# An encoder layer with a product-key expert FFN on one Trainium2 core: the first G load moved to GpSimd's queue, SyncE in written order in the main loop, the next U split ahead of the gathers

## The chip, the cores and the metric

The kernel runs on one core of one Trainium2 chip. The metric is the time of one execution in microseconds on the device. The engines are TensorE (PE; its weight loads are PEld), VectorE (DVE), ScalarE (ACT), GpSimd (POOL) and SyncE (SP), which here only issues DMAs. Line numbers such as L923 are those of the kernel before.

## The reference

One encoder layer for 512 tokens of width 1024: neighbourhood attention and latent attention, a projection and LayerNorm, and then the part that the change touches, a FFN of 128 x 128 experts of which each token takes 16 for each of 8 heads.

```python
def one_chunk(xb):                      # 128 tokens
    q = (xb @ w_q).reshape(PEER_CHUNK, PEER_HEADS, PEER_KEY_DIM)
    s1 = jnp.einsum('thd,kd->thk', q[..., :half], sub_keys[0])
    s2 = jnp.einsum('thd,kd->thk', q[..., half:], sub_keys[1])
    ...                                 # top 16 of the sums: expert numbers idx, weights g
    u = u_table[idx]
    hpre = jnp.einsum('td,ted->te', xb, u)
    act = g * jax.nn.gelu(hpre, approximate=False)
    return jnp.einsum('te,ted->td', act, v_table[idx])
...
h = layer_norm(DN_ALPHA * h + ffn + ple, ln2_g[i], ln2_b[i])
```

## The kernel before

The 16,384 experts are handled as 128 blocks of 128. Tokens 128 to 511 (384 of them) are computed densely: every block's V rows are multiplied with a matrix of activations that is zero where a token did not choose the expert. The routing weights of these tokens, spread out over all experts, are the matrix G, which an earlier stage (`build_g`) writes to DRAM as `g_dram`. Tokens 0 to 127 are computed sparsely, by gathering rows of U and V.

**Ahead of the main loop** (until about 770 us) `route` finds the experts of each token, `build_g` writes G, and a filler computes the first 44 (LEAD) blocks of `expert_in`: the U block of 128 experts is loaded (`raw`, three buffers, L630) and multiplied with 320 tokens (L632, 16 records for each block in full float32), and ScalarE applies Gelu into `ge` (L634). For a while after that, `i_sel` (L776) holds the expert numbers of the sparse tokens.

**The main loop** (L986) goes over the 128 blocks in the order 24 to 127, then 0 to 23; n counts the steps. In a step:
- `expert_in(n + LEAD)` while n + 44 < 128: `stream` loads a U block into `raw` (L87), `split` makes a high part `whi` on ScalarE (L79) and a low part `wlo` on VectorE (L80), both with two buffers, and TensorE runs 24 matmuls of 128x320 into `hp` (two buffers). Gelu follows on ScalarE.
- `load_g` every 8 steps (GB), at n % 8 == 4: one DMA (L923) brings G for eight blocks, 1536 KB, into `gt0` or `gt1` in turn. The first such load, `load_g(0)`, is written ahead of the loop (L933). Its rows in DRAM are cut into runs of 512 bytes, 3072 of them (128 partitions x 24).
- `load_v(n)` loads a V block of 512 KB into `v_raw` (three buffers, L929), and `split` makes `v_hi` and `v_lo`.
- VectorE multiplies G with `ge` in place (L1013), and `split` makes `a_hi` and `a_lo`. For the last 24 steps `ge` comes back from DRAM as `ge_in` (L1008).
- `expert_out`: 18 matmuls of 128x512 into six accumulators `acc` that live through the whole loop.
- Two or three of the 257 gather steps: an indirect DMA of 128 rows by GpSimd into `gat` (six buffers) and one VectorE operation on it (`scr`, L955, for U; `base`, L966, for V). `spent` counts steps, 0.25 for each step without an `expert_in`, so that the gather steps are spread evenly up to n = 115.

After the loop the four row blocks are normalised and stored (L1034 to L1042). Row block 0, the sparse one, is ready when its last gather is, so its normalisation is placed by the planner inside the loop.

**The order of the work.** The program is compiled with a planner that estimates when each instruction can run and orders the instructions of each engine by that. Inside `tc.manual_schedule(engines={...})` the engines named keep the order in which the code is written; before, this is VectorE alone. TensorE, ScalarE, SyncE and GpSimd follow the planner. Each engine then executes its list in order, and an instruction that waits holds up everything behind it on its engine.

In what follows u42 is the load of the U block with number 42 in that sequence (the filler's last two are u42 and u43, the loop's first is u44), W44 the VectorE half of the split of block 44, v3 and V3 the load and the VectorE half of the split of the V block of step 3, gt3 the product in place, A3 the VectorE half of the split of the activations, G0 the first G load and G1 the next, and g one gather's VectorE operation.

Of the kernel before, what the change touches and what calls it, by code (L numbers as in the profile page):

```python
# [32 lines left out]
GT = 16  # L33
GB = 8
LEAD = 44
# [7 lines left out]
NA_KEYS = 256  # L43
NA_FROM = (0, 64, 192, 256)
GATS = 6
LOW = -3.0e38
FEED_NA = 2.75
FEED_LAT = 1.0
# [7 lines left out]
def tile_encoder_layer(ctx: ExitStack, tc: tile.TileContext, A: dict, out: bass.AP):  # L56
    nc = tc.nc
# [15 lines left out]
    def r32(ap):  # L73
        return ap.bitcast(F32)

    def split(hi, lo, src, scale=None):

        if scale is None:
            nc.scalar.copy(hi, src)  # L79
            nc.vector.tensor_tensor(lo, src, r32(hi), op=OP.subtract)  # L80
        else:
            nc.scalar.mul(hi, src, scale)
            nc.vector.scalar_tensor_tensor(lo, src, scale, r32(hi), op0=OP.mult, op1=OP.subtract)

    def stream(src, shape, scale=None):
        raw = wst.tile([128] + shape, F32, name="raw", bufs=3)
        nc.sync.dma_start(raw, src)  # L87
        hi = wst.tile([128] + shape, F32R, name="whi")
        lo = wst.tile([128] + shape, F32R, name="wlo")
        split(hi, lo, raw, scale)  # L90
        return hi, lo

    def mm3(ps, a, b, start, stop):
        nc.tensor.matmul(ps, a[0], b[0], start=start, stop=False)  # L94
        nc.tensor.matmul(ps, a[0], b[1], start=False, stop=False)  # L95
        nc.tensor.matmul(ps, a[1], b[0], start=False, stop=stop)  # L96
# [85 lines left out]
    def soft(s_in, p, nk, mx, scale=1.0, minus=-1.0):  # L182

        nmx = small.tile([128, 1], F32, name="nmx")
        nc.vector.tensor_scalar(nmx, mx, minus, None, op0=OP.mult)
        sm = small.tile([128, 1], F32, name="sm")
        nc.scalar.activation(p[:, :nk], s_in, AF.Exp, bias=nmx, scale=scale, accum_out=sm)
        rs = small.tile([128, 1], F32, name="rs")
        nc.vector.reciprocal(rs, sm)
        nc.vector.tensor_scalar(p[:, :nk], p[:, :nk], rs, None, op0=OP.mult)  # L190
# [52 lines left out]
    with tc.tile_pool(name="ln0", bufs=1, reuse_waits="tile") as ln0:  # L243
# [5 lines left out]
        for c in range(4):  # L249
            layer_norm(h[c], eg, eb)  # L250
            transpose_to(hTh, hTl, h[c], c)
            if c == 0:
                for kk in range(4):
                    raw = wst.tile([128, 2, 512], F32, name="raw", bufs=3)
# [141 lines left out]
    def na_scores(m, b, hh):  # L396
# [9 lines left out]
        nc.vector.tensor_tensor_reduce(p[:, :NA_KEYS], ps[:, :NA_KEYS], bias, op0=OP.add, op1=OP.max,  # L406
                                       accum_out=mx, scale=1.0, scalar=LOW)
        soft(p[:, :NA_KEYS], p, NA_KEYS, mx)
# [203 lines left out]
    g_dram = dram.tile([NTG, 128, 128 * GT], F32, name="g_dram")  # L612
# [7 lines left out]
    def expert_in(i, whole=None):  # L620


        ps = psH.tile([128, 512], F32, name="hp")
        if whole is None:
            u = stream(A["uT"][i], [8, 128])
            for k in range(8):
                mm3(ps[:, :N_U], (u[0][:, k], u[1][:, k]), (hTh[:, k, ts], hTl[:, k, ts]), k == 0, k == 7)
        else:
            u = wst.tile([128, 8, 128], F32, name="raw", bufs=3)
            nc.sync.dma_start(u, A["uT"][i])  # L630
            for k in range(8):
                nc.tensor.matmul(ps[:, :N_U], u[:, k], whole[:, k, :], start=(k == 0), stop=(k == 7))  # L632
        ge = pB.tile([128, N_U], F32, name="ge", bufs=LEAD - SPILL + 2)
        nc.scalar.activation(ge, ps[:, :N_U], AF.Gelu)  # L634
        if i < SPILL:
            nc.sync.dma_start(ge_dram[i], ge)
        else:
            ge_t[i] = ge
# [14 lines left out]
    def top16(vals, idx, src, tmp):  # L653
        nc.vector.max(vals[:, 0:8], src)
        nc.vector.max_index(idx[:, 0:8], vals[:, 0:8], src)
        nc.vector.match_replace(tmp, vals[:, 0:8], src, LOW)
        nc.vector.max(vals[:, 8:16], tmp)
# [258 lines left out]
    order = list(range(SPILL, 128)) + list(range(SPILL))  # L916
    pV = ctx.enter_context(tc.tile_pool(name="pV", bufs=1, side="right", reuse_waits="tile"))

    def load_g(n):
        i = order[n]  # L920
        t = pV.tile([128, NTG, GB, GT], F32, name="gt0") if n // GB % 2 == 0 else pE.tile([128, NTG, GB, GT], F32,
                                                                                          name="gt1", bufs=1)
        nc.sync.dma_start(t.rearrange("p g i t -> p g (i t)"),  # L923
                          g_dram[:, :, i * GT:(i + GB) * GT].rearrange("g p x -> p g x"))
        return t

    def load_v(n):
        raw = pV.tile([128, D], F32, name="v_raw", bufs=3)
        nc.sync.dma_start(raw, v_rows[order[n] * 128:(order[n] + 1) * 128, :])  # L929
        return raw  # L930

    v_next = [load_v(n) for n in range(2)]
    gt_next = load_g(0)  # L933
    v_next.append(load_v(2))
    for c in range(NGC):
        for _ in route(c, []):
# [14 lines left out]
    def gather_u(c, k):  # L951
        u = pG.tile([128, D], F32, name="gat", bufs=GATS)
        nc.gpsimd.indirect_dma_start(out=u[:], out_offset=None, in_=u_rows,  # L953
                                     in_offset=bass.IndirectOffsetOnAxis(ap=i_sel[:, c, k:k + 1], axis=0))
        nc.vector.scalar_tensor_tensor(scr, u, 1.0, h[c], op0=OP.mult, op1=OP.mult,  # L955
                                       accum_out=hdot[:, c, k:k + 1])
# [5 lines left out]
    def gather_v(c, k):  # L962
        u = pG.tile([128, D], F32, name="gat", bufs=GATS)
        nc.gpsimd.indirect_dma_start(out=u[:], out_offset=None, in_=v_rows,  # L964
                                     in_offset=bass.IndirectOffsetOnAxis(ap=i_sel[:, c, k:k + 1], axis=0))
        nc.vector.scalar_tensor_tensor(base[c], u, hdot[:, c, k:k + 1], base[c], op0=OP.mult, op1=OP.add)  # L966

    def gather_steps():
        for c in range(NGC):
            for k in range(128):  # L970
                yield lambda c=c, k=k: gather_u(c, k)
            yield lambda c=c: gather_act(c)
            for k in range(128):
                yield lambda c=c, k=k: gather_v(c, k)

    def expert_out(x, c, halves=(0, 1)):
        n, ah, al, vh, vl = x
        cs = slice(c * 128, (c + 1) * 128)
        for hf in halves:
            hs = slice(hf * 512, (hf + 1) * 512)  # L980
            mm3(acc[c][hf], (ah[:, cs], al[:, cs]), (vh[:, hs], vl[:, hs]), n == 0, n == 127)

    steps = list(gather_steps())
    done, spent = 0, 0
    late = []
    with tc.manual_schedule(engines={nc.vector.engine}):  # L986
        for n, i in enumerate(order):
            if n + LEAD < 128:
                expert_in(n + LEAD)
            if n % GB == 0:  # L990
                gt = gt_next
            if n % GB == GB // 2 and n + GB // 2 < 128:
                gt_next = load_g(n + GB // 2)
            raw = v_next[n] if n < 3 else load_v(n)
            if n in (124, 125):
                vh = wst.tile([128, D], F32R, name="whi")
                vl = wst.tile([128, D], F32R, name="wlo")
                a2 = wst.tile([128, 2, N_D], F32R, name="raw", bufs=3)
                ah, al = a2[:, 0], a2[:, 1]
            else:  # L1000
                vh = pP.tile([128, D], F32R, name="v_hi")
                vl = pP.tile([128, D], F32R, name="v_lo")
                ah = pP.tile([128, N_D], F32R, name="a_hi")
                al = pP.tile([128, N_D], F32R, name="a_lo")
            split(vh, vl, raw)
            if i < SPILL:
                ge = pG.tile([128, N_U], F32, name="ge_in", bufs=2)
                nc.sync.dma_start(ge, ge_dram[i])  # L1008
            else:
                ge = ge_t.pop(i)  # L1010
            a = gt[:, :, n % GB, :]
            dn = gt[:, N_S // GT:, n % GB, :]
            nc.vector.tensor_tensor(dn, dn, ge.rearrange("p (g t) -> p g t", t=GT), op=OP.mult)  # L1013
            split(ah.rearrange("p (g t) -> p g t", t=GT), al.rearrange("p (g t) -> p g t", t=GT), a)
            late.append((n, ah, al, vh, vl))
            if n < 124:
                for c in range(NDC):
                    expert_out(late[0], c)
                late = []
            spent += 1 if n + LEAD < 128 else 0.25  # L1020
            upto = min(len(steps), math.ceil(len(steps) * spent / (128 - 0.75 * LEAD - 3)))
            for f in steps[done:upto]:
                f()
            done = upto
        for c in range(NDC):
            for hf in range(2):
                for x in late:
                    expert_out(x, c, (hf,))


    lg = row_bcast(pG, A["ln2_g"], "gat", GATS)
    lb = row_bcast(pG, A["ln2_b"], "gat", GATS)
    for c in range(4):
# [96 lines left out]
```

## Time and profile before

| | us |
|---|---|
| median of 3 runs | 1614.23 |
| lowest and highest | 1613.36, 1614.41 |
| the profiled execution | 1615.94 |
| its span, first to last instruction | 1613.6 |
| TensorE busy, whole span | 1555.9 |
| TensorE busy from 740 to 800 us | 49.94 of 60 |
| TensorE busy from 800 to 1560 us | 760.00 of 760 |
| VectorE busy from 800 to 1560 us | 649.40 of 760 |
| mean DMA rate from 800 to 1560 us | 338 GB/s |

The span is what the profile covers; the execution's own time is 2.3 us longer. Rows of the timeline give start, duration, engine, line, operation, the tile written and those read, and in square brackets the idle time of the engine before it with what ended it. Rows of the stage view give the stretch, its length, for PE, PEld, DVE, ACT and POOL the busy time with the number of records, and then the clock that was granted to TensorE, the DMA engines' busy share and GB/s.

### The profile page before, as it was taken

The page shows a single profiled execution, that of the slowest core. Times are in us where ns is not written, and L with a number is a line of the kernel's source. Part 1 is how long each engine was busy: PE and PEld are TensorE (multiplying, and loading weights), DVE is VectorE, ACT ScalarE, POOL GpSimd, SP SyncE. Part 2 cuts the span into 40 slices and gives each one's busy share as a digit, 9 for nine tenths or more (in the row PEclk, how much of TensorE's full clock was granted, in tenths as well). Part 3 has the DMA queues.
Part 4 walks back from the last instruction along what each step waited for, and adds up shares of the span by engine and source line. Part 5 has one row for each costly group of instructions (what it writes and reads, how often), then busy time and mean ns, then how long its engine had stood idle before and what let it go on. Part 6 is the DMA issues. An engine that isn't in the chain of part 4 may idle for free.

```text
span 1613.6 us, 23598 instructions
## 1 busy us (share of the span) xinstructions
PE 1555.9 (96%) x8195; PEld 1311.7 (81%) x8195; DVE 1335.7 (83%) x2959; ACT 680.3 (42%) x1190; POOL 530.6 (33%) x407
## 2 busy tenths in 40 slices
PE   6999899999999999999899999999999999999997
PEld 4788677888776776787799999999999999988885
DVE  7366795689999999999588898888888888867776
ACT  3355684433232543675233333333333333333343
POOL 1023000000104444400465665454555555533100
PEclk9999999999999999999899999999999999999999
DMA  7243230332339998957999999999999999977863
GB/s 225 62 116 91 82 119 27 113 87 79 105 129 338 351 360 291 344 216 261 322 342 365 372 360 386 362 345 355 352 337 369 367 333 373 348 246 256 286 223 112
DMA packets 192887, 411.75 MB, mean 255 GB/s; under 512 B 14848, under 2 KB 103296, under 8 KB 189696
## 3 DMA queue, kind: packets, MB, share of 16 engines
q1 hardware_dynamic: 144000, 236.68, 42.8%
q0 software_dynamic: 48768, 173.56, 29.2%
q8 instruction: 65, 1.06, 0.3%
q14 instruction: 54, 0.44, 0.1%
HBM read 373.95 MB, written 33.29 MB: 252 GB/s over the span
## 4 chain that ended last, share of the span: by engine, by line
PE 76%; DVE 15%; DMA 5%; issue 2%; ACT 1%; SPq 1%; POOL 1%; DVEq 0%; ACTq 0%; POOLq 0%
PE acc L96 11%; PE acc L95 11%; PE acc L94 11%; PE hp L94 6%; PE hp L96 6%; PE hp L95 6%; DVE oh_j L804 4%; PE pj L94 3%; PE pj L95 3%; PE mm L94 3%; PE pj L96 3%; PE mm L95 3%; PE mm L96 3%; DMA whi<-in_u_rows_dram,s_sel 2%; PE hp L632 2%
## 5 line engine op out<-in xcount | busy, mean ns | idle before, releaser
L96 PE MATMUL acc<-v_hi,a_lo 128*128 128x512 f32 x756 | 295.6, 391 | 0.0
L95 PE MATMUL acc<-v_lo,a_hi 128*128 128x512 f32 x756 | 294.7, 390 | 0.0
L94 PE MATMUL acc<-v_hi,a_hi 128*128 128x512 f32 x756 | 294.4, 390 | 0.0
L964 POOL DMA_INDIRECT gat<-in_v_rows_dram,i_sel x128 | 203.3, 1588 | 198.5 <-DVE base L966 167.7
L953 POOL DMA_INDIRECT gat<-in_u_rows_dram,i_sel x128 | 189.8, 1483 | 238.0 <-DVE scr L955 114.3
L79 ACT CAST v_hi<-v_raw 128x1024 fp32r<-128x1024 f32 x126 | 132.4, 1051 | 217.2 <-issue 170.3
L96 PE MATMUL hp<-hTh,wlo 128*128 128x320 f32 x672 | 207.8, 309 | 6.8 <-DVE wlo L80 6.8
L94 PE MATMUL hp<-hTh,whi 128*128 128x320 f32 x672 | 208.3, 310 | 0.0
L95 PE MATMUL hp<-hTl,whi 128*128 128x320 f32 x672 | 207.7, 309 | 0.0
L632 PE MATMUL hp<-whole,raw 128*128 128x320 f32 x704 | 204.2, 438 | 3.6 <-DMA raw<-in_uT_dram 3.6
L79 ACT CAST whi<-raw 128x1024 fp32r<-128x1024 f32 (+3 forms) x137 | 138.3, 1009 | 149.0 <-PE mm L95 49.3
L80 DVE TENSOR_TENSOR wlo<-raw,whi 128x1024 fp32r<-128x1024 f32 (+3 forms) x137 | 160.5, 1172 | 38.4 <-ACT whi L79 37.9
L80 DVE TENSOR_TENSOR v_lo<-v_raw,v_hi 128x1024 fp32r<-128x1024 f32 x126 | 154.2, 1224 | 36.6 <-ACT v_hi L79 35.5
L632 PEld LDWEIGHTS hp<-whole,raw 128*128 128x128 f32 x704 | 130.6, 193 | 51.4 <-issue 7.1
L79 ACT CAST a_hi<-gt 128x384 fp32r<-128x384 f32 x126 | 64.6, 513 | 253.8 <-DVE gt L1013 252.8
L955 DVE SCALAR_TENSOR_TENSOR scr<-gat,h 128x1024 f32<-128x1024 f32 x128 | 156.5, 1223 | 15.8 <-DMA gat<-in_u_rows_dram,i_sel 13.0
L96 PEld LDWEIGHTS acc<-v_hi,a_lo 128*128 128x128 f32 x756 | 141.9, 188 | 31.2 <-DVE a_lo L80 1.7
L966 DVE SCALAR_TENSOR_TENSOR base<-gat,hdot,base 128x1024 f32<-128x1024 f32 x128 | 164.1, 1282 | 2.4
L94 PEld LDWEIGHTS acc<-v_hi,a_hi 128*128 128x128 f32 x756 | 141.9, 188 | 27.3 <-ACT a_hi L79 0.7
L95 PEld LDWEIGHTS acc<-v_lo,a_hi 128*128 128x128 f32 x756 | 141.9, 188 | 26.4
L80 DVE TENSOR_TENSOR a_lo<-gt,a_hi 128x384 fp32r<-128x384 f32 x126 | 70.3, 558 | 83.5 <-ACT a_hi L79 83.5
L96 PEld LDWEIGHTS hp<-hTh,wlo 128*128 128x128 f32 x672 | 127.0, 189 | 7.1 <-DVE wlo L80 7.0
(343 smaller groups left out, 2871.9 us busy)
## 6 DMA issues: line engine op xcount, KB each, us to landing
raw<-in_uT_dram SPq DMA_DIRECT2D x128, 512.0 KB, 6.8
v_raw<-in_v_rows_dram SPq DMA_DIRECT2D x128, 512.0 KB, 7.5
g_dram<-g_st SPq DMA_DIRECT2D x24, 1024.0 KB, 5.0
gt<-g_dram SPq DMA_DIRECT2D x16, 1536.0 KB, 15.2
raw<-in_w_in_dram SPq DMA_DIRECT2D x17, 512.0 KB, 3.8
raw<-in_w_q_dram SPq DMA_DIRECT2D x16, 512.0 KB, 3.9
na_b<-in_na_bias_dram POOLq DMA_DIRECT2D x32, 128.0 KB, 2.4
raw<-in_w_o_dram SPq DMA_DIRECT2D x8, 512.0 KB, 3.6
```

What stands on the lines that cost most here:

```text
L79: nc.scalar.copy(hi, src)
L80: nc.vector.tensor_tensor(lo, src, r32(hi), op=OP.subtract)
L94: nc.tensor.matmul(ps, a[0], b[0], start=start, stop=False)
L95: nc.tensor.matmul(ps, a[0], b[1], start=False, stop=False)
L96: nc.tensor.matmul(ps, a[1], b[0], start=False, stop=stop)
L632: nc.tensor.matmul(ps[:, :N_U], u[:, k], whole[:, k, :], start=(k == 0), stop=(k == 7))
L804: nc.vector.tensor_scalar(oj[:, i], iota, eT[:, 1, t0 + i:t0 + i + 1], eT[:, 2, t0 + i:t0 + i + 1], op0=OP.is_equal, op1=OP.mult)
L953: nc.gpsimd.indirect_dma_start(out=u[:], out_offset=None, in_=u_rows, in_offset=bass.IndirectOffsetOnAxis(ap=i_sel[:, c, k:k + 1], axis=0))
L955: nc.vector.scalar_tensor_tensor(scr, u, 1.0, h[c], op0=OP.mult, op1=OP.mult, accum_out=hdot[:, c, k:k + 1])
L964: nc.gpsimd.indirect_dma_start(out=u[:], out_offset=None, in_=v_rows, in_offset=bass.IndirectOffsetOnAxis(ap=i_sel[:, c, k:k + 1], axis=0))
L966: nc.vector.scalar_tensor_tensor(base[c], u, hdot[:, c, k:k + 1], base[c], op0=OP.mult, op1=OP.add)
```

## The change

There are four edits, all in the main loop or just ahead of it.

1. G0 is issued from GpSimd's queue instead of SyncE's.
2. SyncE joins VectorE in the manual schedule: in the loop its DMAs are issued in written order.
3. `expert_in(44)` is written ahead of the loop, and each step's `expert_in`, now that of the next step, stands behind `expert_out` and ahead of the gathers. The split of V moves behind the product with G.
4. No gather steps in the first two steps (NO_GATHER); the divisor is made smaller by 2, so that the last gather stays at n = 115.

```diff
+NO_GATHER = 2
...
-    def load_g(n):
+    def load_g(n, queue=nc.sync):
...
-        nc.sync.dma_start(t.rearrange("p g i t -> p g (i t)"),
-                          g_dram[:, :, i * GT:(i + GB) * GT].rearrange("g p x -> p g x"))
+        queue.dma_start(t.rearrange("p g i t -> p g (i t)"),
+                        g_dram[:, :, i * GT:(i + GB) * GT].rearrange("g p x -> p g x"))
...
-    gt_next = load_g(0)
+    gt_next = load_g(0, nc.gpsimd)
...
-    with tc.manual_schedule(engines={nc.vector.engine}):
+    with tc.manual_schedule(engines={nc.vector.engine, nc.sync.engine}):
+        expert_in(LEAD)
         for n, i in enumerate(order):
-            if n + LEAD < 128:
-                expert_in(n + LEAD)
...
-            split(vh, vl, raw)
             if i < SPILL:
...
             nc.vector.tensor_tensor(dn, dn, ge.rearrange("p (g t) -> p g t", t=GT), op=OP.mult)
+            split(vh, vl, raw)
             split(ah.rearrange("p (g t) -> p g t", t=GT), al.rearrange("p (g t) -> p g t", t=GT), a)
...
-            spent += 1 if n + LEAD < 128 else 0.25
-            upto = min(len(steps), math.ceil(len(steps) * spent / (128 - 0.75 * LEAD - 3)))
+            if n + 1 + LEAD < 128:
+                expert_in(n + 1 + LEAD)
+            if n >= NO_GATHER:
+                spent += 1 if n + LEAD < 128 else 0.25
+            upto = min(len(steps), math.ceil(len(steps) * spent / (128 - 0.75 * LEAD - 3 - NO_GATHER)))
```

The lists of instructions of the two programs differ as follows. VectorE, before: W44 V0 gt0 A0 g g g, W45 V1 gt1 A1 g g g, and so on; after: W44, gt0 V0 A0 W45, gt1 V1 A1 W46, gt2 V2 A2 W47 g g g, gt3 V3 A3 W48 g g g, and so on. SyncE, before: v0 v1 G0 v2 u42 u43 u44 u45 u46 v3 u47 G1, two `ge_in`, u48 v4 u49; after: v0 v1 v2 u42 u43 u44 u45 u46 u47 v3 u48 G1 v4 u49. Each later G load stands one U and one V load later than before. GpSimd has G0 ahead of all the gathers of the loop. ScalarE, after: W44, Gelu of block 42, a_hi of step 0, W45, Gelu of block 43, a_hi of step 1, W46. TensorE's list is the same up to the order of some matmuls of one group.

Two more places are ordered differently. Row block 0's normalisation: before, VectorE's list is g, statistics, V115 gt115, statistics, A115, aggregate, first product of the normalisation (L132), V116 gt116, reciprocal and three small operations, A116, one small operation, second product (L135), V117; after, it is g, gt115, both statistics, V115 A115 gt116, aggregate, L132, reciprocal, four small operations, L135, V116 A116 gt117. On ScalarE the square root of it comes behind the V116 split before, and ahead of it after. At the very end, the last row sum (L1039) is followed before by row block 3's mean and by the second product of row block 2 beside it; after, that second product (L135) stands between the row sum and the mean.

## The prediction

> **What bounds the kernel now.** I read the page first, then the stages around the main loop, then TensorE's timeline where it is not full, then what the late engines waited for. Page and stages:
>
> ```profile
> PE 1555.9 (96%) x8195; PEld 1311.7 (81%) x8195; DVE 1335.7 (83%) x2959; ACT 680.3 (42%) x1190; POOL 530.6 (33%) x407
> ```
> ```profile
> 800.00:1560.00 760.00, 760.00 (x4035) 676.35 (x4035) 649.40 (x812) 288.50 (x396) 379.67 (x244) 1.00 0.94 338
> ```
> ```profile
> 750.00:755.00 5.00, 5.00 (x21) 3.50 (x20) 5.00 (x5) 2.33 (x3) 0.00 (x0) 1.00 0.93 302
> ...
> 760.00:765.00 5.00, 1.98 (x5) 1.36 (x6) 4.90 (x4) 0.20 (x1) 0.00 (x0) 0.85 0.80 320
> ...
> 785.00:790.00 5.00, 1.47 (x5) 1.47 (x6) 4.70 (x7) 0.00 (x0) 1.23 (x2) 0.50 1.05 381
> ```
>
> TensorE is the bound, and from 800 to 1560 us it has no idle time at all: nothing done to the loop's body can gain there. It is idle, and then at half its clock (0.50), only where the loop begins. Its timeline there:
>
> ```profile
> 742.87 16.85 PE L632 MATMUL hp<-whole,raw 128*128 128x320 f32 x62
> ```
> ```profile
> 763.02 10.54 PE L632 MATMUL hp<-whole,raw 128*128 128x320 f32 x32 [3.29 <-DMA raw<-in_uT_dram]
> 773.16 0.55 PE L94 MATMUL hp<-hTh,whi 128*128 128x320 f32 x1
> ...
> 776.92 0.39 PE L94 MATMUL acc<-v_hi,a_hi 128*128 128x512 f32 x1
> ...
> 781.02 0.31 PE L94 MATMUL hp<-hTh,whi 128*128 128x320 f32 x1
> ...
> 788.53 0.64 PE L96 MATMUL hp<-hTh,wlo 128*128 128x320 f32 x1 [6.76 <-DVE wlo L80]
> ```
> ```profile
> 794.42 0.39 PE L94 MATMUL acc<-v_hi,a_hi 128*128 128x512 f32 x1
> ```
>
> Two waits: 3.29 us for the U load of block 42, and 6.76 us for W45. What was behind them:
>
> ```profile
> 748.74 0.38 SPq L923 DMA_DIRECT2D gt<-g_dram  x1
> 749.17 7.38 SPq L929 DMA_DIRECT2D v_raw<-in_v_rows_dram  x1
> 756.60 0.90 SPq L630 DMA_DIRECT2D raw<-in_uT_dram  x2
> ...
> 774.01 0.39 SPq L923 DMA_DIRECT2D gt<-g_dram  x1
> 774.45 13.64 SPq L1008 DMA_DIRECT2D ge_in<-ge_dram  x2
> ```
> ```profile
> 751.15 0.44 ACT L634 ACTIVATE ge<-hp 128x320 f32<-128x320 f32 x1 [0.30 <-PE hp L632]
> ...
> 764.72 0.29 DVE L776 SCALAR_TENSOR_TENSOR i_sel<-e,e 128x128 int32<-128x128 f32 x1
> ...
> 774.41 0.94 POOL L953 DMA_INDIRECT gat<-in_u_rows_dram,i_sel  x1 [8.19 <-ACT ge L634]
> ```
> ```profile
> 784.57 1.23 DVE L955 SCALAR_TENSOR_TENSOR scr<-gat,h 128x1024 f32<-128x1024 f32 x1 [12.71 <-DMA gat<-in_u_rows_dram,i_sel]
> ...
> 787.26 1.21 DVE L80 TENSOR_TENSOR wlo<-raw,whi 128x1024 fp32r<-128x1024 f32 x1
> ```
>
> The issue that follows G0 on SyncE is held for 7.38 us, so u42 goes out at 756.60, though its buffer was free when block 39 was done, by 751.15. And VectorE stood 12.71 us in a gather of step 0 with W45 behind it in its list.
>
> **Part by part: the start.** Let TensorE run on without a gap from the end of block 41, 742.87 + 16.85 = 759.72. Blocks 42 and 43 are 32 records at 16.85/62 = 0.272 us: 8.7. The 24 matmuls of block 44 took 773.16 to 776.92: 3.76, and block 45 the same. Step 0's products took 776.92 to 781.02: 4.10. Together 20.3 us, where 794.42 - 759.72 = 34.7 went by. The most the start can give is 14.4 us: 10.05 idle (3.29 + 6.76), the rest slow clock. Each gap needs its supply.
>
> u42 (edit 1): with v2 ahead of it but no G0, it goes at 751.2. Loads of this line took:
>
> ```profile
> DMA to landing us min/median/max: 3.4/4.0/7.0
> ```
>
> It lands by 758.2 at the worst, before 759.72; u43, freed 4.3 us (16 records) later, likewise. The 3.29 goes.
>
> W45 (edit 3) stands ahead of the first gather. Block 42 ends at 764.1 and frees a buffer; u45 lands 4 to 7 us later, by 771.1; the two halves of the split take 1.05 and 1.21: 773.4. TensorE wants it at 759.72 + 8.7 + 3.76 + 4.10 = 776.3, so 2.9 us of cover. W46 and W47 have their turn before a gather too (steps 0 and 1 have none, edit 4). The first g stands after W47, which waits for block 45 to free `whi` (780); TensorE then still has steps 1 to 3 to do, and wants V3 at 768.4 + 3 x 7.86 + 3.76 = 796. So a gather that lands as late as in the row above (10 us after its issue) stops nobody. The 6.76 goes.
>
> G0 on GpSimd's queue is the one operation that the trace does not show: a copy of 3072 runs whose addresses are made by GpSimd. It can be issued when G is stored, as on SyncE, at 748.7. What VectorE does behind it (product, V0, A0):
>
> ```profile
> L80 DVE TENSOR_TENSOR v_lo<-v_raw,v_hi 128x1024 fp32r<-128x1024 f32 x126 | 154.2, 1224 | 36.6 <-ACT v_hi L79 35.5
> ...
> L80 DVE TENSOR_TENSOR a_lo<-gt,a_hi 128x384 fp32r<-128x384 f32 x126 | 70.3, 558 | 83.5 <-ACT a_hi L79 83.5
> ...
> L1013 DVE TENSOR_TENSOR gt<-gt,ge 128x320 f32<-128x320 f32 x104 | 50.2, 483 | 0.0
> ```
>
> That is 2.27 us, and TensorE's first product is due at 759.72 + 8.7 + 3.76 = 772.2, so landing by 770 costs nothing. The nearest rows for the copy:
>
> ```profile
> L399 POOL DMA_DIRECT2D na_b<-in_na_bias_dram x32: 536/538/735, 5.9 to 156.9; - x32
> ...
> DMA to landing us min/median/max: 2.2/2.4/6.4
> ```
> ```profile
> L953 POOL DMA_INDIRECT gat<-in_u_rows_dram,i_sel x128: 939/1804/2005, 765.3 to 1108.6; - x128
> ```
> ```profile
> L923 SPq DMA_DIRECT2D gt<-g_dram x16: 377/377/386, 748.7 to 1533.4; - x16
> ...
> DMA to landing us min/median/max: 8.2/15.2/20.2
> ```
>
> Lower bound: SyncE's best, 8.2 us, landing at 757. Upper bound: 128 rows of a gather in 1.804 us are 14.1 ns each, 43.3 us for 3072, landing with 2.4 more at 794. I take the direct copy, the same kind of instruction with no indices to read: 0.538/128 = 4.2 ns, 12.9 us, landing at 748.7 + 12.9 + 2.4 = 764. Cost 0, cover 6 us.
>
> The clock: 32 records took 10.54 us after the gap of 3.29 and would take 8.7, at a granted 0.85, so I count 1.8 us of slow clock for that gap. The Trainium skill (TensorE: Matmul & The Clock Gate, section on the HAM clock gate) has the clock halved after an idle window of about 3.4 us; by that the shorter gap would have cost only its idle time and the start would give 12.6. The trace disagrees, and the measurement decides.
>
> **The loop.** 257 steps over 90 counts instead of 92 are 2.86 gathers a step instead of 2.79: 0.07 x 1.23 = 0.09 us of VectorE, which is busy 649.40 of 760, so hidden; a_hi is now made beside V's half, which saves VectorE a wait. Traffic grows by about 1%, and slack shows here (all waits of VectorE for a U gather):
>
> ```profile
> DVE scr L955 <- DMA gat<-in_u_rows_dram,i_sel: 13.0, 2, 12.7
> ```
>
> Both are at the start; later gathers were never late. SyncE's written order (edit 2) moves each later G behind one more U and V load; behind it wait v, u, v, each loaded three steps ahead. Cost 0.
>
> **The end.** Two orders get worse.
>
> ```profile
> 1549.86 1.05 ACT L79 CAST v_hi<-v_raw 128x1024 fp32r<-128x1024 f32 x1 [0.20 <-PE acc L96]
> ```
> ```profile
> 1550.48 1.27 DVE L132 SCALAR_TENSOR_TENSOR base<-base,ln_mu,gat 128x1024 f32<-128x1024 f32 x1
> 1551.67 1.22 DVE L80 TENSOR_TENSOR v_lo<-v_raw,v_hi 128x1024 fp32r<-128x1024 f32 x1
> ...
> 1553.40 0.16 DVE L100 TENSOR_TENSOR ln_t<-ln_ve,ln_y 128x1 f32<-128x1 f32 x1
> ...
> 1554.59 1.28 DVE L135 SCALAR_TENSOR_TENSOR base<-base,ln_y,gat 128x1024 f32<-128x1024 f32 x1
> ```
> ```profile
> 1604.13 0.69 DVE L1039 SCALAR_TENSOR_TENSOR h<-h,acc 128x512 f32<-128x512 f32 x1
> ...
> 1605.12 1.28 DVE L135 SCALAR_TENSOR_TENSOR h<-h,ln_y,gat 128x1024 f32<-128x1024 f32 x1
> 1605.30 1.15 ACT L122 ACTIVATE scr<-h,ln_mu 128x1024 f32<-128x1024 f32 x1 [3.04 <-DVE ln_mu L119]
> ```
>
> In step 116, V116 (1551.67) now stands behind L135 and five small operations like that of 1553.40: 1.28 + about 0.9, less the 0.4 by which L132 comes earlier: it ends near 1554.7 instead of 1552.9. TensorE ended step 114 at 1549.86, ends 115 at 1553.96, and needs V116 one matmul (0.23) later: 0.5, and 0.5 more for A116, so 1.0 us lost (bounds 0, if the sum shifts earlier, and 2). At the end, L135 of row block 2 (1.28) ran beside ScalarE's square at 1605.30; now it stands ahead of it, and the small operations that were spread out come before the row sum of 1604.13: 1.28 + 0.4 = 1.7 us (bounds 1.2 and 1.8).
>
> **Sum.** -14.4 + 0 + 0 + 1.0 + 1.7 = -11.7 us. The profiled execution took 1615.94 for a span of 1613.6; it becomes about 1604.2. The median of the runs is 1.7 lower: 1614.23 - 11.7 = 1602.5.
>
> **Rivals.**
>
> *G0 late by a little* (0.16). At the gather's fastest price, 0.939/128 = 7.3 ns, G0 needs 22.5 us and lands at 773.6; TensorE loses 3.6 and up to 2 of clock: 1606 to 1608. A second way to the same time: VectorE is full until 765.0 (5.00 of 5.00 in the row 750 to 755; i_sel ends at 764.72 + 0.29), and if GpSimd cannot write addresses beside it, G0 lands at 765.0 + 8.2 = 773. For it: gathers took 0.94 us beside an idle VectorE and 1.80 in the median. Against: the direct copies kept 0.538. The Trainium skill (SBUF — State Buffer, section on the two separate sides) warns of just this: GpSimd cannot write DMA descriptors while certain fast VectorE operations hold a port that the two share, and advises SyncE's queue. Whether route's operations are of that kind no run here shows.
>
> *G0 very late* (0.07): 14.1 ns each, landing at 794. TensorE waits 24 us where it waited 10, with slow clock behind it: -11.7 + 24.4 + 2 gives 1629. It is slower from a landing at about 785 on. Against it: the 538 ns.
>
> *Gathers collide* (0.09): six gathers, G0's rest and G1 share the DMA engines near 775 to 790; with G's 20.2 us for the first gather VectorE comes to V3 5 us late: 1607.
>
> *SyncE's order stalls* (0.08): issues were held 13.64 us behind G1 and a load lands 7 later; in the last 44 steps of 4.1 us three steps are only 12.3. If each of the five G loads there costs 2 to 3 us, the gain is gone: 1614, slower if more. Against it: the same five stand in the same stretch now and TensorE is full.
>
> **How the numbers follow.** Forecast 0.60, the rivals as above. Faster by over 0.2% (3.2 us; a smaller change could hardly be told from none here): 0.60 + 0.16 + 0.09 = 0.85. Same: 0.04, half of the last rival. Slower: 0.07 + 0.04 = 0.11. The range goes from the whole start with no loss at the end, 1614.23 - 14.4 = 1599.8, less 0.8 for clock at the edges, 1599, up to 1609, which holds the two milder rivals.
>
> **What would show it.** Right: no PE row with a wait between 755 and 800, the clock at 1.00 there, u42 issued near 751, G0 landed before 770, the first g after W47, and the end longer by 1 to 2 us after the last matmul. Wrong: a wait of gt0 or of a_hi for G0; a PE wait for `v_lo` or `wlo` after a G load; a loop that is not full from 800 to 1540.

## The result and the profile after

| | before | changed |
|---|---|---|
| median of the runs, first series | 1613.80 us | 1600.12 us, ratio 0.9918 (95% interval 0.9901 to 0.9936) |
| median of the runs, second series | 1614.66 us | 1605.97 us, ratio 0.9950 (0.9931 to 0.9969) |
| profiled execution | 1615.94 us, span 1613.6 | 1602.71 us, span 1600.9 |

The change makes the kernel faster, by 13.7 us (0.8%) in one series of runs and 8.7 (0.5%) in the other. The forecast, 1602.5, lies between the two medians, and both lie in the range, 1599 to 1609. The runs of one kernel scatter by up to 14 us, and the profiles differ by up to 6.9 us ahead of the loop, where all kernels run the same instructions in the same order (last section). So kernels are compared here by stage, inside their profiles, and the medians stand beside that.

The page of the changed kernel, and its windows:

```profile
PE 1550.4 (97%) x8195; PEld 1308.8 (82%) x8195; DVE 1332.2 (83%) x2959; ACT 681.0 (43%) x1190; POOL 486.4 (30%) x408
```
```profile
750.00:755.00 5.00, 5.00 (x20) 3.51 (x19) 4.97 (x7) 3.07 (x4) 1.51 (x1) 1.00 0.96 314
...
760.00:765.00 5.00, 5.00 (x21) 3.44 (x20) 4.93 (x3) 0.44 (x1) 0.00 (x0) 1.00 0.94 316
...
785.00:790.00 5.00, 5.00 (x30) 4.63 (x30) 4.29 (x6) 2.39 (x4) 2.96 (x3) 1.00 1.13 321
```

The window 760 to 765, which had 1.98 us of TensorE, and the window 785 to 790, which had 1.47 at a clock of 0.50, are both full now, at 1.00. TensorE's timeline has one run of 94 records where it had 62, a gap and 32:

```profile
743.71 25.47 PE L633 MATMUL hp<-whole,raw 128*128 128x320 f32 x94
```

The supply behind it, from SyncE's queue, GpSimd and VectorE in turn:

```profile
748.42 1.29 SPq L930 DMA_DIRECT2D v_raw<-in_v_rows_dram  x3
751.98 4.63 SPq L631 DMA_DIRECT2D raw<-in_uT_dram  x2
...
772.43 0.70 SPq L924 DMA_DIRECT2D gt<-g_dram  x1
773.59 12.73 SPq L930 DMA_DIRECT2D v_raw<-in_v_rows_dram  x1
```
```profile
752.00 1.51 POOL L924 DMA_DIRECT2D gt<-g_dram  x1 [69.20 <-DMA v_raw<-in_v_rows_dram]
766.14 0.99 POOL L954 DMA_INDIRECT gat<-in_u_rows_dram,i_sel  x1 [12.64 <-DVE i_sel L777]
```
```profile
767.64 1.23 DVE L81 TENSOR_TENSOR wlo<-raw,whi 128x1024 fp32r<-128x1024 f32 x1 [1.78 <-ACT whi L80]
768.78 0.49 DVE L1012 TENSOR_TENSOR gt<-gt,ge 128x320 f32<-128x320 f32 x1
...
770.80 1.23 DVE L81 TENSOR_TENSOR wlo<-raw,whi 128x1024 fp32r<-128x1024 f32 x1
...
782.45 1.22 DVE L956 SCALAR_TENSOR_TENSOR scr<-gat,h 128x1024 f32<-128x1024 f32 x1
```

u42 goes out at 751.98 instead of 756.60. G0 occupies GpSimd for 1.51 us, and VectorE's first product (768.78) follows W44 without waiting for it. W45 is done by 772.03 where it ended at 788.47, and the first gather's operation finds its rows there. What is held 12.73 us behind the second G load is now v4, and TensorE does not wait for it.

The only wait of TensorE between the loop's start and its end, and the end itself on VectorE and ScalarE:

```profile
1575.10 0.51 PE L95 MATMUL acc<-v_hi,a_hi 128*128 128x512 f32 x1 [0.62 <-ACT a_hi L80]
```
```profile
1590.23 0.69 DVE L1042 SCALAR_TENSOR_TENSOR h<-h,acc 128x512 f32<-128x512 f32 x1
...
1590.84 1.28 DVE L136 SCALAR_TENSOR_TENSOR h<-h,ln_y,gat 128x1024 f32<-128x1024 f32 x1
```
```profile
1592.47 1.15 ACT L123 ACTIVATE scr<-h,ln_mu 128x1024 f32<-128x1024 f32 x1 [3.98 <-DVE ln_mu L120]
```

From the last row sum to ScalarE's square it is 2.24 us now; it was 1.17. In the chain of work that ended last, a V load of the last steps stands behind the 0.62 us:

```profile
1567.71 1.15 DVE wlo L81
...
1568.88 4.62 DMA v_raw<-in_v_rows_dram
...
1573.59 1.06 ACT v_hi L80
```

For all kernels I cut the time behind the routing into three stages: **start**, from the first record of the last long run of `hp` matmuls (743.71 above) to the first product of step 3, counted from 0; **loop**, from there to the end of the last matmul; **end**, from there to the span's end. All in us, each from the timeline of one profile:

| kernel | start | loop | end | sum | median of runs |
|---|---|---|---|---|---|
| before | 66.47 | 794.75 | 9.51 | 870.73 | 1612.77 to 1615.25 |
| changed | 51.66 | 794.82 | 10.71 | 857.19 | 1600.12 |
| changed, second profile | 51.98 | 795.60 | 10.69 | 858.27 | 1605.97 |
| edit 1 alone | 59.23 | 796.93 | 9.57 | 865.73 | 1610.15 |
| edits 3 and 4 | 56.73 | 796.72 | 10.59 | 864.04 | 1609.61 |
| edits 2, 3, 4 | 56.52 | 796.15 | 10.57 | 863.24 | 1606.89 |
| edits 1, 3, 4 | 51.93 | 797.51 | 10.64 | 860.08 | 1604.09 |
| edits 1, 2, 3 | 57.76 | 796.16 | 10.66 | 864.58 | 1611.15 |
| edits 1 and 4 | 51.75 | 795.00 | 9.61 | 856.36 | 1599.90 |

Of the 12.70 us between the spans of the first two rows 14.81 come from the start, -0.07 from the loop, -1.20 from the end, and -0.84 from ahead of all three (742.87 and 743.71). The two profiles of the changed kernel differ by 0.3 us in the start and 0.8 in the loop, so a difference of that size between two rows says nothing.

My theory for the experiments: each gap of the start is a supply that stands behind something in a list, and which edit takes it away can be seen by leaving the edits out one at a time.

### The profile page after: what moved, and what is told of

It is laid out like the page before. It is cut to its first block, busy times and chain, and to the rows that moved or that the text cites. A ratio compares the mean times of both kernels' runs of the same rounds, so it can differ in the third digit from the quotient of the medians.

```text
span 1600.9 us, 23593 instructions
## 1 busy us (share of the span) xinstructions
PE 1550.4 (97%) x8195; PEld 1308.8 (82%) x8195; DVE 1332.2 (83%) x2959; ACT 681.0 (43%) x1190; POOL 486.4 (30%) x408
## 2 busy tenths in 40 slices
DMA packets 190199, 411.75 MB, mean 257 GB/s; under 512 B 14848, under 2 KB 100224, under 8 KB 187008
## 3 DMA queue, kind: packets, MB, share of 16 engines
q8 instruction: 65, 1.06, 0.3%
## 4 chain that ended last, share of the span: by engine, by line
PE 77%; DVE 13%; DMA 4%; issue 3%; ACT 1%; POOL 1%; SPq 0%; DVEq 0%; ACTq 0%; POOLq 0%
PE acc L96 11%; PE acc L97 11%; PE acc L95 11%; PE hp L95 6%; PE hp L96 6%; PE hp L97 6%; PE pj L95 3%; PE pj L96 3%; PE pj L97 3%; PE mm L95 3%; PE mm L96 3%; PE mm L97 3%; PE hp L633 3%; DVE oh_j L805 2%; PE tr L810 2%
## 5 line engine op out<-in xcount | busy, mean ns | idle before, releaser
L965 POOL DMA_INDIRECT gat<-in_v_rows_dram,i_sel x128 | 173.1, 1352 | 220.2 <-DVE base L967 192.0
L954 POOL DMA_INDIRECT gat<-in_u_rows_dram,i_sel x128 | 174.4, 1363 | 179.1 <-DVE scr L956 137.9
L96 PEld LDWEIGHTS hp<-hTl,whi 128*128 128x128 f32 x672 | 126.3, 188 | 3.7
L95 PEld LDWEIGHTS hp<-hTh,whi 128*128 128x128 f32 x672 | 126.0, 187 | 3.3
```

## Experiments

**Edit 1 alone**, on the kernel before:

```diff
-    gt_next = load_g(0)
+    gt_next = load_g(0, nc.gpsimd)
```

> The kernel before with edit 1 alone: G0 through GpSimd's queue, everything else as before. Theory (the two gaps share a cause: u42 late makes block 42's ge late, which makes the first gather late): u42 goes out near 751, the 3.29 us gap goes, and since the first gather waits no more 8.19 us for that ge, it goes near 766 instead of 774.4, so VectorE comes to W45 some 8 us earlier than 788.5: the second gap shrinks from 6.76 to about 4 us without vanishing. Gain 8 to 9 us, 1605 to 1606, and no loss at the end. Rival (the gaps are separate, as my sum had them, 5.1 us for the first with its clock): the second gap keeps its 6.8 us and the gain is 5 us, 1609. Rival (edit 1 does all of it, edit 3 is idle): 1600.

1610.15 us, ratio 0.9970 (0.9957 to 0.9983). TensorE and VectorE at the start:

```profile
742.37 25.57 PE L632 MATMUL hp<-whole,raw 128*128 128x320 f32 x94
...
781.57 0.64 PE L96 MATMUL hp<-hTh,wlo 128*128 128x320 f32 x1 [5.43 <-DVE wlo L80]
```
```profile
777.25 1.22 DVE L955 SCALAR_TENSOR_TENSOR scr<-gat,h 128x1024 f32<-128x1024 f32 x1 [5.59 <-issue]
...
780.29 1.22 DVE L80 TENSOR_TENSOR wlo<-raw,whi 128x1024 fp32r<-128x1024 f32 x1
```

The gap for u42 is gone. The second gather of step 0 now holds VectorE for 5.59 us where it held it for 12.71, and W45 starts at 780.29 instead of 787.26, 7 us earlier, as the theory of a shared cause had it; but TensorE also comes there earlier, so its wait shrinks from 6.76 to 5.43 only. The start gains 7.24 us, which is between the two theories (8 to 9, and 5). The loop is 2.18 us longer than before, 1.45 of them in two waits that I had not expected (0.59 for a split of U near 807, 0.86 for a_hi near 1511), and the median is only 2.6 us under that of the kernel before in the same series.

**Edits 3 and 4 alone**: the changed kernel with `load_g(0)` on SyncE and the manual schedule for VectorE only.

> Edits 3 and 4 alone: next U split ahead of the gathers, gathers from the third block on; G0 on SyncE's queue, SyncE's order not written out. Theory: the gap of 3.29 us for u42 stays with its clock (u42 still held behind G0 and v2 until about 756.6), the 6.76 us of W45 go, the end is longer by 1.1 us: gain of about 8, 1605 to 1607. Together with the run of edit 1 alone the gains would then add to more than the 13.7 us measured for the whole change. Rival (separate gaps): gain 9.3 - 1.5 = 8, the same time, so what tells them apart is the sum with edit 1 alone. Rival (edit 3 is idle without edit 1, as W45's own load u45 is late): the second gap stays in part, 1610.

1609.61 us, ratio 0.9976 (0.9965 to 0.9988). The first gap stays and the second is gone:

```profile
763.75 10.54 PE L633 MATMUL hp<-whole,raw 128*128 128x320 f32 x32 [3.14 <-DMA raw<-in_uT_dram]
```

The start gains 9.74 us, the end loses 1.08, as expected. The loop loses another 2 us in waits that I had not expected; they are those of the run without SyncE's order, below. 7.24 and 9.74 add to 17.0, the whole change has 14.81: the two gaps overlap in their cause.

**All but edit 1**: G0 back on SyncE's queue.

> The changed kernel with G0 back on SyncE's queue (edits 2, 3 and 4). Theory: as edits 3 and 4 alone, 1605 to 1607, with a wait of 3 us for u42 and a slow clock behind it; edit 2 worth nothing. Rival (SyncE's written order is what lets u42 go early, since v2 stands elsewhere): no gap, 1600.

1606.89 us, ratio 0.9966 (0.9951 to 0.9982). The start, 56.52 us, is that of edits 3 and 4 alone (56.73), so SyncE's written order does not release u42:

```profile
757.64 10.54 PE L633 MATMUL hp<-whole,raw 128*128 128x320 f32 x32 [2.92 <-DMA raw<-in_uT_dram]
```
```profile
1540.73 0.73 PE L96 MATMUL acc<-v_lo,a_hi 128*128 128x512 f32 x2 [0.52 <-DVE v_lo L81]
```

The second row is a loss where I forecast one, in step 116: V116 stands behind the norm's last operation. But the product ahead of that norm had also waited 0.83 us for its gate load, which it did not in the changed kernel, so the 0.52 us are not the norm's order alone.

**All but edit 2**, SyncE's order left to the scheduler:

```diff
-    with tc.manual_schedule(engines={nc.vector.engine, nc.sync.engine}):
+    with tc.manual_schedule(engines={nc.vector.engine}):
```

> The changed kernel without SyncE's written order (edits 1, 3 and 4). Theory (edit 2 is worth nothing; its order differs from the scheduler's only in where a G load and a few gate loads stand): 1600, within 1.5 us of the changed kernel, no gap from 755 to 1540; the gate loads of blocks 104 and 105 go early and the late V load near step 126 may come a little earlier or later, 0.6 us. Rival (the written order keeps the U loads ahead of the gate loads and that matters): a gap of 2 us or more at the loop's start, 1603 or more.

1604.09 us, ratio 0.9940 (0.9921 to 0.9959). The start is the changed kernel's, but the loop is 2.69 us longer than in its first profile and 1.91 longer than in its second. TensorE, VectorE and SyncE's queue there:

```profile
1498.26 0.50 PE L95 MATMUL acc<-v_hi,a_hi 128*128 128x512 f32 x1 [1.30 <-ACT v_hi L80]
1499.52 0.50 PE L96 MATMUL acc<-v_lo,a_hi 128*128 128x512 f32 x1 [0.76 <-DVE v_lo L81]
```
```profile
1496.15 0.49 DVE L1012 TENSOR_TENSOR gt<-gt,ge_in 128x320 f32<-128x320 f32 x1 [4.49 <-DMA ge_in<-ge_dram]
1498.24 1.22 DVE L81 TENSOR_TENSOR v_lo<-v_raw,v_hi 128x1024 fp32r<-128x1024 f32 x1 [1.60 <-ACT v_hi L80]
```
```profile
1483.71 0.38 SPq L924 DMA_DIRECT2D gt<-g_dram  x1
1485.31 3.59 SPq L1007 DMA_DIRECT2D ge_in<-ge_dram  x1
```

The scheduler has put a G load ahead of the gate load of step 106. That gate load is held 3.59 us behind it and lands late, the product waits 4.49 us for it, and V's split, which edit 3 has put behind the product, waits with it. In the written order the first gate loads go before this G load, and the product of step 106 does not wait. That of step 108 does there, 1.60 us (3.17 in the second profile), but TensorE loses nothing by it (0.16). So the theory that edit 2 is worth nothing falls, and so does the rival, which had it worth something at the loop's start: it is worth 1.9 to 2.7 us, and 2.06 of them are the two waits at step 106.

**The changed kernel again**, unaltered, in one series with the next three.

> The changed kernel once more, unaltered, beside the next three kernels: 1600 to 1602. From the end of the routing matmuls to the third step 51.7 us as in its first profile, 14.8 less than before; 0 to 1 us of waits of TensorE after that; 10.7 us behind the last matmul. What differs from the first profile should lie ahead of 740 us, where both kernels are the same.

1605.97 us, where 1600 to 1602 was expected. The three stages agree with the first profile within 0.8 us each (table above), and the last `hp` run starts at 741.83 instead of 743.71. Its profiled run took 1601.84 us, which is the shortest of the series, so the profile shows nothing of what made the second median 5.9 us longer than the first (the last section has the clock of these runs).

**Without edit 4**:

```diff
-NO_GATHER = 2
+NO_GATHER = 0
```

> The changed kernel with gathers from the first block on (edit 4 undone). Theory: W45 is split before the first gather lands, so the 6.76 us stay gone; but the first gather, issued near 766, lands near 776, three of them keep VectorE until 780 and the product, V1 and A1 of step 1 stand behind them: TensorE waits 1 to 1.5 us near 780 and about 1 us again in step 2; 1602 to 1603. Rival (edit 4 carries what edit 3 seems to give): a wait of 5 us or more, 1606. Rival (edit 4 is idle, the gathers land in time): no wait, as the changed kernel.

1611.15 us, ratio 0.9971 (0.9958 to 0.9985). W45 is in time, but step 1 is not. TensorE, VectorE and the windows:

```profile
785.53 0.80 PE L95 MATMUL acc<-v_hi,a_hi 128*128 128x512 f32 x1 [4.17 <-ACT a_hi L80]
```
```profile
780.49 1.23 DVE L956 SCALAR_TENSOR_TENSOR scr<-gat,h 128x1024 f32<-128x1024 f32 x1 [6.24 <-DMA gat<-in_u_rows_dram,i_sel]
...
784.45 0.49 DVE L1012 TENSOR_TENSOR gt<-gt,ge 128x320 f32<-128x320 f32 x1
```
```profile
785.00:790.00 5.00, 4.47 (x13) 3.34 (x14) 4.96 (x6) 1.76 (x3) 1.67 (x2) 0.66 1.07 367
```

The second gather lands near 780, the third near 783, and the product of step 1 stands behind both: 4.17 us of waiting and slow clock (0.66) behind it. The start is 6.1 us longer than with edit 4. I had expected 2 to 3; the rival, with a wait of 5 us or more, was nearer. That made me doubt that edit 3 does anything at the start.

**Edits 1 and 4 alone**, everything else as before:

```diff
-    gt_next = load_g(0)
+    gt_next = load_g(0, nc.gpsimd)
...
-            spent += 1 if n + LEAD < 128 else 0.25
+            if n >= NO_GATHER:
+                spent += 1 if n + LEAD < 128 else 0.25
...
```

> The kernel before with edits 1 and 4 alone: G0 through GpSimd's queue and gathers from the third block on, but the U split still behind the gathers, V's split ahead of the product and SyncE's order left to the scheduler. My prediction gave the 6.76 us of W45 to edit 3. Rival theory after the run without edit 4 (which lost 6.1 us up to the third step): edit 4 alone takes the gathers from in front of W45 and W46, W47 is wanted only near 792 and the gathers have landed by 780, so edit 3 is idle at the loop's start: from the end of the routing matmuls to the third step 51.7 to 52 us as in the changed kernel. Prediction's theory: W47 behind three gathers is late, 2 us or more above 52. After that up to 1.5 us of waits near 1500, as the run of edit 1 alone has 0.86 us there; end 9.5 us as before. Time 1600 to 1603.

1599.90 us, ratio 0.9916 (0.9884 to 0.9947). TensorE has no wait that the profile shows from the routing to the last matmul, not even the one near 1500 that I had allowed for:

```profile
740.00:800.00 60.00, 60.00 (x291) 49.46 (x290) 49.81 (x111) 21.64 (x31) 17.84 (x15) 1.00 0.96 335
800.00:1560.00 760.00, 760.00 (x4013) 674.64 (x4012) 648.65 (x810) 290.69 (x397) 371.17 (x242) 1.00 0.93 338
```
```profile
776.46 1.22 DVE L956 SCALAR_TENSOR_TENSOR scr<-gat,h 128x1024 f32<-128x1024 f32 x1
...
780.14 1.22 DVE L81 TENSOR_TENSOR wlo<-raw,whi 128x1024 fp32r<-128x1024 f32 x1
```

Three gathers stand ahead of W47 (780.14) and it is early enough; the gathers have landed when VectorE comes to them. The start is 51.75 us, that of the whole change, and the end 9.61, that of before. Edits 1 and 4 bring the whole gain. Beside them edit 3 adds nothing at the start and costs 1.1 us at the end, and edit 2 mends a wait that edit 3 brings in. Without edit 4, edit 3 brings 1.5 us (59.23 with edit 1 alone, 57.76 with 1, 2 and 3): it lets W45 through, and TensorE then waits for step 1's product instead.

**V's split ahead of the product again**, without SyncE's written order (edits 1, 4 and half of 3):

```diff
+            split(vh, vl, raw)
             if i < SPILL:
...
             nc.vector.tensor_tensor(dn, dn, ge.rearrange("p (g t) -> p g t", t=GT), op=OP.mult)
-            split(vh, vl, raw)
```

> The changed kernel without SyncE's written order and with V's split ahead of the product again (edits 1, 4 and half of 3). The run without SyncE's order waited 1.30 + 0.76 us near 1498, where the product waited 4.49 us for a gate load that stands behind a G load on SyncE, and V's split stood behind the product. Theory (V's split behind the product turns the late gate load into two waits): with V's split ahead, only a_hi is late: 0.9 us or less in place of 2.06, as in the run of edit 1 alone (0.86). Rival (the late gate load alone sets it): 2 us as there.

1601.06 us, ratio 0.9912 (0.9881 to 0.9943); start 51.68, loop 794.85, end 9.58. No wait of TensorE is left near 1498, and the product of step 106 has none either:

```profile
1496.77 1.23 DVE L81 TENSOR_TENSOR v_lo<-v_raw,v_hi 128x1024 fp32r<-128x1024 f32 x1 [0.96 <-ACT v_hi L80]
1497.91 0.49 DVE L1013 TENSOR_TENSOR gt<-gt,ge_in 128x320 f32<-128x320 f32 x1
```

So the wait at step 106 takes both: the scheduler's order on SyncE and V's split behind the product. With the split ahead, VectorE asks for the gate only at 1497.91. How much of the 2.06 us is the split's place stays open: the gate load is also held less here (1.63 us behind the G load, 3.59 there), and with edit 1 alone, where V's split stands ahead too, a late gate load costs 0.86 us. The end's 1.1 us hang on the place of V's split: this kernel differs from the run without SyncE's order in nothing else, and its end is 9.58 where that one's is 10.64.

**Two repairs on the changed kernel**: the end's order written out, and the last two V loads in gather buffers.

```diff
-        raw = pV.tile([128, D], F32, name="v_raw", bufs=3)
+        raw = pG.tile([128, D], F32, name="gat", bufs=GATS) if n >= 126 else pV.tile([128, D], F32, name="v_raw", bufs=3)
...
+            if n == 118:
+                lg = row_bcast(pG, A["ln2_g"], "gat", GATS)
+                lb = row_bcast(pG, A["ln2_b"], "gat", GATS)
...
+        z[0](1)   # last row sum of row block 3
+        z[1]()    # its mean, and the square on ScalarE
+        q[3]()    # second product of row block 2
```

> The changed kernel with two repairs: VectorE's order after the last matmul written out, with the second product of row block 2 behind the mean of row block 3 (it then lies beside ScalarE's square), and the V loads of steps 126 and 127 into gather buffers that are free by then, the final norm's scale and shift loaded at step 118. Theory: the last row sum to the square shrinks from 2.24 us to about 1.1, the end from 10.7 to 9.5 us, and the wait of 0.62 us near 1575 goes: 1.5 to 1.8 us under the changed kernel in the same session, about 1598.5 to 1599. Rival (the end is bound by ScalarE's chain or the store, not by VectorE's order): the end stays at 10.7 us, gain 0.6 at the most. Rival (the rewritten list makes TensorE wait in the last steps): no gain.

1601.59 us, ratio 0.9925 (0.9903 to 0.9947); start 51.67, loop 795.58, end 9.65. The end gains 1.06 us, as expected, and the 0.62 us near 1575 are gone. But the three stages add to 856.90, only 0.3 us under the first profile of the changed kernel, where 1.5 to 1.8 was expected: loading the scale at step 118 made the norm of row block 0 wait 2.10 us for it in front of V's half, and TensorE lost 1.09 us:

```profile
1539.30 0.49 PE L96 MATMUL acc<-v_lo,a_hi 128*128 128x512 f32 x1 [1.09 <-DVE v_lo L81]
```
```profile
1535.81 1.28 DVE L133 SCALAR_TENSOR_TENSOR base<-base,ln_mu,gat 128x1024 f32<-128x1024 f32 x1 [2.10 <-DMA gat<-in_ln_g_dram]
```

**That norm in VectorE's idle stretches** of steps 117 to 121 as well, with its scale loaded at step 116:

```diff
             nc.vector.tensor_tensor(dn, dn, ge.rearrange("p (g t) -> p g t", t=GT), op=OP.mult)
+            first_norm(n)   # 117 statistics, 118 and 120 small operations, 119 and 121 the two products
```

> The changed kernel with three repairs: the end's order written out and the two last V loads in gather buffers as in the run with these two, and the first row block's norm written into VectorE's idle 2 us of steps 117 to 121, its scale and shift loaded at step 116. Theory: the 1.09 us for v_lo near 1539, where the norm waited 2.10 us for its scale, goes too; no wait of TensorE of over 0.3 us after the loop's start, loop 809.7 to 809.9 us from the second step to the last matmul, end 9.65 us: span 2 us under the changed kernel with the same time ahead of the loop. Rival (VectorE's idle stretches there are needed for V's halves): waits of 0.5 us or more in steps 117 to 122.

1602.08 us, ratio 0.9928 (0.9903 to 0.9953); start 51.92, loop 793.85, end 9.57, together 855.34: 1.85 us under the changed kernel's first profile and the shortest of all. TensorE has no wait behind the routing that the profile shows, so the rival falls. The medians do not show the gain: they are 1600.12 and 1605.97 for the changed kernel, 1599.90 for edits 1 and 4, and 1602.08 here. All three beat the kernel before; which of them is best the runs do not settle.

**All G loads on GpSimd's queue**:

```diff
-    def load_g(n, queue=nc.sync):
+    def load_g(n, queue=nc.gpsimd):
```

> The changed kernel with all 16 G loads on GpSimd's queue instead of the first alone. Theory (the copy costs GpSimd 1.5 us each, SyncE's queue is no longer held 5 to 13 us behind a G load, TensorE was full anyway): within 1.5 us of the changed kernel, each G issue about 1.5 us, no held issue on SyncE longer than a buffer takes. Rival (a G load on GpSimd stands ahead of gathers and waits for its buffer, or its runs are written slowly while VectorE is busy): gathers land late, VectorE waits for them, TensorE waits 1 us or more at each of 15 loads: 1610 or more.

1603.12 us, ratio 0.9916 (0.9897 to 0.9935); start 51.76, loop 795.01, end 10.98. The loads by source line:

```profile
L924 POOL DMA_DIRECT2D gt<-g_dram x16: 1473/1482/1503, 753.0 to 1519.6; - x16
...
DMA to landing us min/median/max: 11.2/13.8/20.8
```

Each occupies GpSimd for 1.48 us, and the longest issue of a V load on SyncE is 0.42 us where it was 12.73, so it was the G loads that held SyncE's queue. TensorE is as full as with 15 of them there: the held issues behind the later G loads were covered anyway.

## Why the prediction was right, and where it was not

- **Start, -14.4**: measured -14.81. To the first product of step 1 it was 15.13 (51.55 and 36.42), more than I had called the most: blocks 42 and 43 take 8.2 us where I counted 8.7, and block 45 takes 3.5 where I counted 3.76. Of that 0.32 was given back, since the kernel before ran its next two steps in 7.46 us each instead of 7.62. The mechanism, supply and not TensorE's work, was right for both gaps.
- **Which edit takes the second gap** was wrong. The prediction said that W45 comes in time because edit 3 puts it ahead of the first gather, and gave edit 4 the smaller part. Edits 1 and 4 without 3 have the whole gain, edit 3 without 4 loses 6.1 us of it. The step that failed: I checked that W45 is early, and not whether it would be early without edit 3, once no gather stands ahead of it. The number came out because the kernel has both edits; for edit 3 that was luck. Nor did the sum see that the gaps share a cause, as edit 1 alone shows.
- **G0, cost 0**: right, with a wrong price. I took 4.2 ns for each of 3072 runs; 1.51 us are 0.49 ns. It was issued at 752.0 and not at 748.7; the profile puts its wait down to a V load. Both rivals on G0's price (landing at 773 and 794) fall with the product at 768.78 that did not wait. The second way to the milder one falls too: GpSimd issued it in 1.51 us in a window where VectorE was busy for 4.97 of 5.00. The rule of the Trainium skill behind it (SBUF — State Buffer, two separate sides) says that certain fast VectorE operations keep GpSimd from writing descriptors; no run here shows such a delay.
- **The loop, 0**: measured +0.07. But "SyncE's written order, cost 0" hid a term: against the kernel without that order it is worth 1.9 to 2.7 us, which edit 3 would have cost. The two cancel, and I saw neither, so the 0 is luck in part.
- **Step 116, +1.0**: no wait there in the changed kernel, 0.52 us in the run without edit 1. The term was too large, and 0.62 us that I had not forecast came near 1575.
- **The end, +1.7**: measured 1.20 behind the last matmul, and 1.07 from the last row sum to the square; just the lower bound. The product of 1.28 us was the price; the 0.4 us for the small operations weren't paid.
- **Sum**: the parts that the change touches make -13.54 (-14.81 + 0.07 + 1.20) where the forecast had -11.7. The 1.8 us are the terms above: 0.4 at the start, 0.9 in the loop, 0.5 at the end.
- **Gathers collide** did not happen (782.45 without a wait); **SyncE's order stalls** did not happen either: TensorE stalls in the run without that order.

## What to carry to other kernels

A stall is credited to one of several edits only when each has been left out in turn: here the smallest of four, two steps without gathers, did what the reordering was credited with, and the reordering alone moved the stall to the next step. Where an order is rewritten on one engine, read which load the operation that moved forward now asks for earlier, and where that load stands in its queue. And where the runs scatter more than an edit can bring, cut the profiles at landmarks that all kernels share, and compare the stages.

## What the hardware showed that was not expected

**A copy through GpSimd's queue can be cheap.** It occupied GpSimd for 1.48 us for 3072 runs of 512 bytes, where I had worked out 12.9 us from a copy of 128 rows in 0.54 us: the price is no constant for each run. In the list of DMA queues, with all G loads there, 40,320 fewer packets move than with one (149,879 in all against 190,199), for the same 411.75 MB:

```profile
DMA packets 149879, 411.75 MB, mean 257 GB/s; under 512 B 14848, under 2 KB 54144, under 8 KB 146688
```
```profile
DMA packets 190199, 411.75 MB, mean 257 GB/s; under 512 B 14848, under 2 KB 100224, under 8 KB 187008
```

The first line is that of all G loads on GpSimd's queue, the second the changed kernel's. 15 loads less of 3072 small packets are 46,080, just the difference of those under 2 KB, and 5,760 packets of 2 to 8 KB come in their place, 384 of 4 KB for each load of 1536 KB: the runs of 512 bytes move there in larger packets.

**The clock falls for stretches of 3.41 us, and what a wait costs depends on where it lies.** After waits of 3.29, 3.14 and 2.92 us the next 32 records took 10.54 us each time, where 32 of the 94 without a gap take 8.67. In the kernel before, the wait leaves TensorE busy for 0.50 us of one stretch of 3.41, and the next stretch is at half clock:

```profile
760.11:763.52 3.41, 0.50 (x2) 0.45 (x3) 3.38 (x2) 0.09 (x1) 0.00 (x0) 1.00 0.99 394
763.52:766.93 3.41, 3.41 (x8) 2.06 (x7) 1.90 (x3) 1.04 (x1) 0.94 (x1) 0.50 0.15 62
```

In the traces of all 13 profiles such stretches, up to the last matmul, last 3.41 us or a multiple (10.24 behind the wait of 6.76), and within one profile they start whole multiples of 3.41 us apart. So there is a grid of windows, and it lies differently in each profile. Here is one and the same wait near 173 us in the first profile of the changed kernel, where it lies inside one window, and in the second, where it spans two:

```profile
175.54 0.72 PE L95 MATMUL pj<-cqh,whi 128*128 128x512 f32 x1 [2.46 <-DVE hTl L81]
```
```profile
172.18:175.59 3.41, 0.94 (x5) 0.46 (x3) 3.38 (x7) 2.76 (x6) 2.67 (x6) 1.00 0.71 213
175.59:179.00 3.41, 3.41 (x8) 2.71 (x9) 0.99 (x2) 0.00 (x0) 1.26 (x3) 0.50 0.97 231
```
```profile
175.62 0.47 PE L95 MATMUL pj<-cqh,whi 128*128 128x512 f32 x1 [2.48 <-DVE hTl L81]
```
```profile
170.79:174.21 3.42, 2.36 (x10) 1.43 (x8) 2.79 (x6) 2.70 (x6) 1.21 (x3) 1.00 0.52 163
174.21:177.62 3.41, 2.00 (x9) 1.67 (x10) 2.17 (x4) 0.87 (x2) 2.73 (x6) 1.00 0.92 246
177.62:181.03 3.41, 3.41 (x22) 2.93 (x21) 2.35 (x6) 2.73 (x6) 0.00 (x0) 1.00 0.91 263
```

The first leaves TensorE busy for 28% of a window, and the next window is slow; the second leaves 69 and 59%, and nothing follows. Counted over the windows of this grid from 150 to 1585 us in the 13 profiles, the 38 at full clock in which TensorE was busy for 40.6% or less were all followed by a slow one, and of the 5,373 others, from 40.8% up, none was. (The ends of matmuls are modelled, so the shares are not exact.) The two waits of 1.30 and 0.76 us in the run without SyncE's order left 61% of their window, and the clock stayed.

The Trainium skill (TensorE: Matmul & The Clock Gate, section on the HAM clock gate) has the clock halved after an idle window of about 3.4 us and calls the window free-running. The stretches of 3.41 us agree with that; but here a window with up to 40% of work in it was enough, and the measurement decides.

**Equal code ahead of the loop takes unequal time.** The start of the last `hp` run lay between 737.86 us (all but edit 1) and 744.75 (all G loads on GpSimd), and the earlier of the two profiles has one slow window between 150 and 740 us, the later three. Whole runs go with the clock too: in the seven runs of the changed kernel's second series the mean granted clock was 0.995 in the shortest (1601.84 us), 0.993 in the median and 0.989 in the longest (1612.16). The clock is not all of it: of the runs with the two repairs one of 1600.52 us and one of 1607.30 have the same 0.995. That the place of the grid makes most of the difference is not shown, since the runs without a profile do not show where they lost their clock.
